# One level of Strassen's scheme for the large products of a streaming encoder layer, in three token groups

## The chip, the cores and the metric

The kernel runs on one core of one Trainium2 chip. The metric is the device time of one execution in microseconds. Three timed runs of the kernel before gave 2399.98, 2401.68 and 2405.52 us, median 2401.68.

## What is computed

One mixer layer over 2048 prompt tokens of one stream and 8 x 16 sample tokens, 1024 channels, all in float32. Cut to what matters:

```python
h = rmsnorm(x, norm_w) * (1.0 + scale) + shift            # scale, shift, gate = silu(c) @ w_ada + b_ada
q, k, v, r, a_lr, u, gv, z, g_a, g_b = split(h @ w_in)     # 1024 x 8208
o, S_new = gla_chunked(q, k, v, log_a, S0)                 # linear attention, 4 heads, carried state
y_a = (rmsnorm(o, gla_norm_w) * silu(r)) @ w_proj_a        # 1024 x 1024
s = mix(layernorm(gv))                                     # 128 x 128 matrices over positions
y_b = (u * s * silu(z)) @ w_proj_b                         # 1024 x 1024
x = x + gate * ((sigmoid(g_a) * y_a + sigmoid(g_b) * y_b) @ w_out)   # 1024 x 1024
y = rmsnorm(x, final_norm_w)
```

The large products are those with `w_in` and the three 1024 x 1024 matrices: 2176 tokens (17 tiles of 128) by 1024 by about 11,264 columns, and 16 columns more for `a_lr`.

## The kernel before, in words

**Split operands.** A float32 product is taken as three products in the format `fp32r`: every operand is split into a rounded `hi` and a rest `lo`, and `hi hi + hi lo + lo hi` is summed in PSUM. For a weight block ACT casts (L177) and DVE or POOL subtracts (L178, `wl<-wr,wh`), in quarters of 128x512.

**Loops.** There are five groups of token tiles (4, 4, 3, 3, 3; the sample tile is in the second). A group goes over all weights once, in 44 blocks of 1024 x 256, so that every weight is loaded and split five times. Two forms of product stand in the code: `nat_slot` (L318 to L320: tokens stationary, 256 weight columns moving; for r, v, gv and the output product) and `tr_slots` (L340 to L342: weights stationary, the group's 384 or 512 tokens moving; for the rest). The group's operands (`h`, the attention output, the gated gMLP product, the merged branches) stay in SBUF, already split.

**Order.** The program is written out in its order by Python. `run_block` cuts a weight block's products in slots of 12 (`nat_slot`) or 6 (`tr_slots`), two or four of which fill a bank; before each slot it lets the queue of side work (`Side`) take one step and gives out a quarter of the next block's split. Side work is the linear attention (`gla_gen`), the position mixing (`smix_gen`), the norm and split of the next group's `h` (`stats_gen`, `h_gen`). Every engine runs its own instructions strictly in the order written. The output of a slot lies in one of three PSUM banks (`psg`) until ACT or DVE has taken it out (the `*_evac` functions).

**Fallback.** `body(tc, io, True)` is the path that runs; a flag computed on the chip decides whether the slower `body(tc, io, False)` repeats everything.

## Time and profile before

| | |
|---|---|
| median of three timed runs | 2401.68 us |
| profiled execution, first to last instruction (span) | 2394.5 us |
| what lies around the span, median less span | 7.2 us |
| PE (matmul) busy | 2328.8 us, 97%, 14928 instructions |
| DVE busy | 1004.0 us, 42%, 1935 |
| ACT busy | 920.9 us, 38%, 2015 |
| POOL busy | 965.8 us, 40%, 1085 |
| DMA | 296.91 MB, mean 124 GB/s |
| mean granted TensorE clock | 0.990 of 2.4 GHz |

The page gives no time of the profiled execution beyond its span, so the median stands for it. Matmul times are modelled and overlap: a product of 256 columns is listed with 290 ns although the next one starts 120 ns later. How dense PE works is therefore read from the starts in a timeline, not from the busy share.

### The profile page before, as it was taken

What the parts mean: (1) busy time and instruction counts of PE and PEld (TensorE: products, weight loads), DVE (VectorE), ACT (ScalarE), POOL (GpSimd) and SP (SyncE); (2) the same over time, 40 slices, a digit from 0 to 9 for tenths busy, and PEclk for the clock granted to TensorE, in tenths of its full rate; (3) what the DMA queues carried; (4) which work ended last, traced back from release to release, by engine and by line L of the source; (5) the groups of instructions that cost most, each with busy time, mean ns of one, the idle gap of its engine ahead of it and who ended that gap; (6) DMA issues with size and microseconds to landing.
All of it is one profiled execution on the core that took longest, in us unless ns stands there. A gap on an engine that the chain in (4) does not pass through costs nothing. (4 is left out here: it accounts for less than half of the span.)

```text
span 2394.5 us, 38041 instructions
## 1 busy us (share of the span) xinstructions
PE 2328.8 (97%) x14928; PEld 2183.6 (91%) x14928; DVE 1004.0 (42%) x1935; ACT 920.9 (38%) x2015; POOL 965.8 (40%) x1085
## 2 busy tenths in 40 slices
PE   6999999999999999999999999999999999999998
PEld 4889988889988878888999999999999999999998
DVE  3356522236367432215456322546523264752323
ACT  3344322333434322333455334445433445533342
POOL 3323323344422222435634344563434365433445
PEclk9999999999999999999999999999999999999999
DMA  7643324443444343444444445554445546443543
GB/s 232 177 103 74 91 95 96 98 144 128 127 108 116 95 126 91 97 126 154 134 106 98 123 117 135 189 142 107 98 123 124 168 150 148 94 115 119 125 141 125
DMA packets 286512, 296.91 MB, mean 124 GB/s; under 512 B 10593, under 2 KB 273561, under 8 KB 286322
## 3 DMA queue, kind: packets, MB, share of 16 engines
q1 hardware_dynamic: 282994, 286.74, 44.4%
q10 hardware_dynamic: 2112, 4.19, 0.5%
q0 software_dynamic: 1216, 3.44, 0.4%
q8 instruction: 119, 1.95, 0.3%
q14 instruction: 71, 0.58, 0.1%
HBM read 277.82 MB, written 16.52 MB: 123 GB/s over the span
## 5 line engine op out<-in xcount | busy, mean ns | idle before, releaser
L178 POOL TENSOR_TENSOR wl<-wr,wh 128x512 fp32r<-128x512 f32 (+1 forms) x440 | 579.2, 1318 | 912.4 <-ACT wh L177 864.4
L340 PE MATMUL pg<-u,wh 128*128 128x384 f32 (+1 forms) x2240 | 809.2, 361 | 2.7 <-DVE redo L1028 2.7
L342 PE MATMUL pg<-u,wl 128*128 128x384 f32 (+1 forms) x2240 | 800.0, 357 | 0.0
L341 PE MATMUL pg<-u,wh 128*128 128x384 f32 (+1 forms) x2240 | 799.4, 357 | 0.0
L318 PE MATMUL pg<-wh,u 128*128 128x256 f32 (+1 forms) x2144 | 622.1, 290 | 0.0
L319 PE MATMUL pg<-wl,u 128*128 128x256 f32 (+1 forms) x2144 | 610.1, 285 | 3.4 <-DVE wl L178 2.1
L320 PE MATMUL pg<-wh,u 128*128 128x256 f32 (+1 forms) x2144 | 609.5, 284 | 0.0
L177 ACT CAST wh<-wr 128x512 fp32r<-128x512 f32 (+1 forms) x880 | 512.5, 618 | 209.3 <-issue 89.3
L178 DVE TENSOR_TENSOR wl<-wr,wh 128x512 fp32r<-128x512 f32 (+1 forms) x440 | 337.7, 768 | 516.8 <-ACT wh L177 513.3
L340 PEld LDWEIGHTS pg<-u,wh 128*128 128x128 f32 x2240 | 421.7, 188 | 37.4 <-issue 4.3
L342 PEld LDWEIGHTS pg<-u,wl 128*128 128x128 f32 x2240 | 421.3, 188 | 35.8
L341 PEld LDWEIGHTS pg<-u,wh 128*128 128x128 f32 x2240 | 421.7, 188 | 33.5 <-issue 0.5
L318 PEld LDWEIGHTS pg<-wh,u 128*128 128x128 f32 x2144 | 412.5, 192 | 6.1 <-issue 3.0
L319 PEld LDWEIGHTS pg<-wl,u 128*128 128x128 f32 x2144 | 413.0, 193 | 5.4 <-DVE wl L178 2.3
L320 PEld LDWEIGHTS pg<-wh,u 128*128 128x128 f32 x2144 | 412.7, 193 | 0.0
L1105 POOL TENSOR_TENSOR s<-s,u 128x128 f32<-128x128 f32 x136 | 76.3, 592 | 67.6 <-ACT s L1102 67.6
L353 POOL TENSOR_SCALAR st<-st 128x1 f32<-128x1 f32 x119 | 29.9, 252 | 150.3 <-ACT s L818 93.3
L1079 ACT ACTIVATE u<-pg,ptf 128x384 f32<-128x384 f32 (+1 forms) x40 | 25.0, 625 | 165.5 <-PE pg L342 165.5
L650 POOL TENSOR_TENSOR u<-u,gnwf 128x256 f32<-128x256 f32 x68 | 56.4, 833 | 72.2 <-ACT u L647 69.8
L1084 DVE TENSOR_TENSOR u<-pg,u 128x384 f32<-128x384 f32 (+1 forms) x40 | 24.4, 611 | 134.7 <-PE pg L342 134.7
L1196 POOL TENSOR_TENSOR u<-u,yt 128x256 f32<-128x256 f32 x67 | 55.0, 824 | 56.7 <-DVE yt L1195 56.6
L177 ACT CAST u<-s 128x384 fp32r<-128x384 f32 (+1 forms) x40 | 22.2, 556 | 138.0 <-DVE s L1112 138.0
(202 smaller groups left out, 1964.7 us busy)
## 6 DMA issues: line engine op xcount, KB each, us to landing
wr<-w_in SPq DMA_DIRECT2D x270, 512.0 KB, 5.2
wr<-w_in SPq DMA_DIRECT2D x80, 256.0 KB, 6.0
wr<-w_proj_a SPq DMA_DIRECT2D x40, 512.0 KB, 3.4
wr<-w_proj_b SPq DMA_DIRECT2D x40, 512.0 KB, 3.4
wr<-w_out SPq DMA_DIRECT2D x40, 512.0 KB, 3.4
u<-x_prompt SPq DMA_DIRECT2D x32, 512.0 KB, 6.2
u<-w_ada SPq DMA_DIRECT2D x16, 512.0 KB, 9.0
o_yp<-u SPq DMA_DIRECT2D x15, 512.0 KB, 3.5
```

What stands on the lines that cost most here:

```text
L177: act.copy(hi, src)
L178: eng.tensor_tensor(lo, src, hi.bitcast(F32), ALU.subtract)
L318: pe.matmul(o, ahi(k)[:, t], hi[:, k, 0:w], start=k == 0, stop=False)
L319: pe.matmul(o, ahi(k)[:, t], lo[:, k, 0:w], start=False, stop=False)
L320: pe.matmul(o, alo(k)[:, t], hi[:, k, 0:w], start=False, stop=k == 7)
L340: pe.matmul(o, hi[:, k, cs], bhi(k), start=k == 0, stop=False)
L341: pe.matmul(o, hi[:, k, cs], blo(k), start=False, stop=False)
L342: pe.matmul(o, lo[:, k, cs], bhi(k), start=False, stop=k == 7)
L353: pool.tensor_scalar(dst, src, scale, EPS, ALU.mult, ALU.add)
L650: pool.tensor_tensor(d, d, gnw, ALU.mult)
L1105: pool.tensor_tensor(tj, tj, gv(j)[:, c * 128:(c + 1) * 128], ALU.mult)
L1196: (dve if last and n == 3 else pool).tensor_tensor(y(j)[:, cs], y(j)[:, cs], t, ALU.add)
```

## The change

The first path is replaced by `fast_body`; the fallback `body(tc, io, False)` stays.

A weight block of 1024 x 256 and a group's operand are cut into halves both in the contraction (even and odd chunks of 128) and in columns or tokens. Winograd's form of Strassen's scheme then needs seven block products in place of eight, and 15 additions: four sums `T1` to `T4` of weight quarters (POOL, L281 to L287), four sums `S1` to `S4` of operand quarters (`combos`, L220 to L229), and seven sums of the products, taken partly in PSUM (later products are added to a bank that already holds an earlier one) and partly by DVE (`evac`, L335 to L339, and the `*_fin` functions).

There are three groups of tiles: 6, 5 (with the sample tile) and 6. All products have weights stationary; half a group's tokens move: 384, 320, 384 columns. A *place* is one of a block's seven products: 12 matmuls into one of the banks R, X, Q. In the program's list of places the first place of a block comes before the last of the block ahead. While place n is issued, the weights of place n+4 are summed, those of n+3 cast and those of n+2 subtracted.

The split operands of a phase (7 quarters and sums, `hi` and `lo`) fill 14 of 18 large tiles, so there is room for one set only. Every operand is therefore written to DRAM as seven float32 sums (`publish`) and, during the last block of the phase ahead, loaded again and split (`build_plan`: 14 pairs of load and fill, 128x768 or 128x640). The gates and the merged first branch also go by way of DRAM. The first group's `h` is summed and split directly in the prologue (`direct`). Between the last projection b and the last output phase, which needs its result, no other phase is left; its operands are built when projection b has ended (`flush`). `v`, `gv` and the output now come out with channels on partitions, and are transposed on PE.

```diff
+AOPS = ("S1", "A11", "S2", "S4", "A12", "S3", "A22")
+BOPS = ("T1", "B11", "T2", "B22", "B21", "T3", "T4")
+PLACE = "RXQRXQQ"
+P_GN, P_NF = 68, 70
+LEAD = 2
...
+    groups = [prompt[0:6], [("s", 0)] + prompt[6:10], prompt[10:16]]
...
+    upool, spool, cpool = pl("u", 18), pl("s", 5), pl("c", 6)
+    rpool, tpool, wpool = pl("wr", 4), pl("wt", 3), pl("w", 6)
...
+    def combos(even, odd, h, eng=None):
+
+        a11, a21, a12, a22 = even[:, 0:h], even[:, h:2 * h], odd[:, 0:h], odd[:, h:2 * h]
+        e = (lambda: eng) if eng is not None else either
+        yield "A11", a11
+        yield "A12", a12
+        yield "A22", a22
+        x1 = CT(h)
+        e().tensor_tensor(x1, a21, a22, ALU.add)
+        yield "S1", x1
+        x2 = CT(h)
+        e().tensor_tensor(x2, x1, a11, ALU.subtract)
+        yield "S2", x2
+        x4 = CT(h)
+        e().tensor_tensor(x4, a12, x2, ALU.subtract)
+        yield "S4", x4
+        x3 = CT(h)
+        e().tensor_tensor(x3, a11, a21, ALU.subtract)
+        yield "S3", x3
+
+    def publish(st, kp, even, odd, eng=pool):
+        for o, src in combos(even, odd, st.h, eng):
+            sync.dma_start(st.d[o, kp // 2][:, kp % 2, :], src)
+            yield
+
...
+        def add(self, o):
+            q, sub = self.quarter, ALU.subtract
+            if o == "T1":
+                pool.tensor_tensor(self.t4(o), q("B12"), q("B11"), sub)
+            elif o == "T2":
+                pool.tensor_tensor(self.t4(o), q("B22"), self.tmp["T1"], sub)
+            elif o == "T3":
+                pool.tensor_tensor(self.t4(o), q("B22"), q("B12"), sub)
+                self.t4("T4")
+                pool.tensor_tensor(self.tmp["T4"], q("B21"), self.tmp["T2"], sub)
+
+        def src(self, o):
+            return self.tmp[o] if o[0] == "T" else self.quarter(o)
+
+        def hi(self, o):
+            self.w[o] = wpool.tile([128, 2, 4, 128], F32R, tag="w", name=nm("w"))
+            act.copy(self.w[o][:, 0], self.src(o))
+
+        def lo(self, o):
+            w = self.w[o]
+            (pool if o == "T3" else dve).tensor_tensor(w[:, 1], self.src(o), w[:, 0].bitcast(F32), ALU.subtract)
+
...
+    def evac(b, i):
+
+        blk, bk = blocks[b], banks[b]
+        h = blk.ops.h
+        if i == 1:
+            bk["p1"], bk["t"] = CT(h), CT(h)
+            act.copy(bk["p1"], bk["X"])
+            dve.tensor_tensor(bk["t"], bk["R"], bk["p1"], ALU.add)
+        elif i == 2:
+            bk["u2"] = CT(h)
+            dve.tensor_tensor(bk["u2"], bk["Q"], bk["p1"], ALU.add)
+        elif i == 3:
+            blk.fin(1, 0, bk["R"], bk["u2"])
+        elif i == 4:
+            blk.fin(0, 0, bk["X"], None)
+        elif i == 5:
+            blk.fin(1, 1, bk["Q"], bk["t"])
+        elif i == 6:
+            blk.fin(0, 1, bk["Q"], bk["p1"])
+            if blk.after:
+                blk.after()
+            del banks[b]
+
+    last = [None]
+
+    def flush():
+        if last[0] is not None:
...
+    def run(n):
+        b, i = places[n]
...
+        flush()
+        if i == 4 and b + 2 < len(blocks):
+            blocks[b + 2].load()
+        prepare(n + LEAD + 2, "add")
+        prepare(n + LEAD + 1, "hi")
+        prepare(n + LEAD, "lo")
+        bk, ops = banks[b], blk.ops
+        h = ops.h
+        p = PLACE[i]
+        if i < 3:
+            bk[p] = PSG()[:, 0:h]
+        out, w = bk[p], blk.w[BOPS[i]]
+        hi, lo = ops.t[AOPS[i]]
+        for k in range(4):
+            kw = {"skip_group_check": i > 2}
+            pe.matmul(out, w[:, 0, k, :], hi[:, k, :], start=i < 3 and k == 0, stop=False, **kw)
+            pe.matmul(out, w[:, 0, k, :], lo[:, k, :], start=False, stop=False, **kw)
+            pe.matmul(out, w[:, 1, k, :], hi[:, k, :], start=False, stop=k == 3, **kw)
+            if k % 2:
+                step()
+        del blk.w[BOPS[i]]
+        last[0] = (b, i)
+
+
+    class Phase:
+        def __init__(self, g, st, blks, spare, flush=False):
...
+    def build_plan(ph):
+
+        out = []
+        for o in AOPS:
+            for q in range(2):
+                def load(o=o, q=q, box={}):
+                    t = S(2 * ph.ops.h).rearrange("p (k t) -> p k t", k=2)
+                    sync.dma_start(t, ph.set.d[o, q])
+                    ph.box[o, q] = t
+
+                def fill(o=o, q=q):
+                    if q == 0:
+                        ph.ops.alloc(o)
+                    ph.ops.fill(o, slice(2 * q, 2 * q + 2), ph.box.pop((o, q)), pool if q else dve)
+                out.append((load, fill))
+        ph.box = {}
...
+            blk.ops = ph.ops
+            blocks.append(blk)
+    held = {ph.first for ph in phases if ph.flush}
+    for b in range(len(blocks)):
+        if b in held:
+            places.append((b - 1, 6))
+        places.append((b, 0))
+        if b and b not in held:
+            places.append((b - 1, 6))
+        places += [(b, i) for i in range(1, 6)]
+    places.append((len(blocks) - 1, 6))
...
         with tc.manual_schedule():
-            body(tc, io, True)
+            fast_body(tc, io)
```

**On PE**, at a switch from one product chain to the next in a product with weights stationary (first group, `pg` is the PSUM bank; `u` the split operand; `wh`, `wl` or `w` the split weights). Before:

```order
L342 MATMUL pg_3867<-u_374,wl_3755 128x512
L340 MATMUL pg_3867<-u_374,wh_3754 128x512
L341 MATMUL pg_3867<-u_376,wh_3754 128x512
L342 MATMUL pg_3867<-u_374,wl_3755 128x512
L340 MATMUL pg_3906<-u_230,wh_3826 128x512
L341 MATMUL pg_3906<-u_232,wh_3826 128x512
```

With the change, where place 6 of one block (`A22` with `T4`, added into bank Q) ends and place 1 of the next (`A11` with `B11`, bank X) begins:

```order
L381 MATMUL pg_5874<-u_720,w_5912 128x384
L382 MATMUL pg_5874<-u_721,w_5912 128x384
L383 MATMUL pg_5874<-u_720,w_5912 128x384
L381 MATMUL pg_5993<-u_470,w_5932 128x384
L382 MATMUL pg_5993<-u_471,w_5932 128x384
L383 MATMUL pg_5993<-u_470,w_5932 128x384
```

A chain of 24 matmuls of 512 columns has become a place of 12 of 384. The first place adds into a bank that DVE has read twice before, and the bank of the second was last read after place 4 of the block ahead.

**On POOL**, in projection b of the first group (`wl`, `w`: `lo` of weights; `wt`: sums of weights; `u_4299` and `u_7910`: the merged branch; `c`: sums for the operand of the output product). Before:

```order
L178 TENSOR_TENSOR wl_4543<-wr_4464,wh_4542 128x512
L1147 TENSOR_TENSOR u_4299<-u_4299,u_3125 128x512
L178 TENSOR_TENSOR wl_4543<-wr_4485,wh_4542 128x512
L1147 TENSOR_TENSOR u_4299<-u_4299,u_3125 128x512
L178 TENSOR_TENSOR wl_4621<-wr_4540,wh_4620 128x512
L1147 TENSOR_TENSOR u_4299<-u_4299,u_3125 128x512
L178 TENSOR_TENSOR wl_4621<-wr_4561,wh_4620 128x512
L1147 TENSOR_TENSOR u_4299<-u_4299,u_3125 128x512
```

With the change (L1194 and L1195 are the gate and the merge, L220 to L229 the operand sums, the others the weights):

```order
L285 TENSOR_TENSOR wt_8102<-wr_7779,wr_7777 128x512
L287 TENSOR_TENSOR wt_8104<-wr_7779,wt_8042 128x512
L281 TENSOR_TENSOR wt_8128<-wr_8021 128x512
L220 TENSOR_TENSOR c_8147<-u_7910 128x384
L298 TENSOR_TENSOR w_8130<-wt_8102,w_8130 128x512
L223 TENSOR_TENSOR c_8161<-c_8147,u_7910 128x384
L226 TENSOR_TENSOR c_8170<-u_7910,c_8161 128x384
L1194 TENSOR_TENSOR u_8059<-u_8059,c_8173 128x384
L1195 TENSOR_TENSOR u_8060<-u_8060,u_8059 128x384
L229 TENSOR_TENSOR c_8190<-u_7910 128x384
L1195 TENSOR_TENSOR u_8060<-u_8060,u_8059 128x384
L283 TENSOR_TENSOR wt_8201<-wr_8023,wt_8128 128x512
```

Between one block's first weight sum (L281) and the next there stood two subtractions and two merges for each slot; now five instructions on weights, seven of the branch and four of the operand sums stand there.

**On DVE**, one token tile's step of the linear attention (first group; `sstf` the state, `am`, `kl`, `sh`, `v` small split operands, `pg` a product's bank). Before:

```order
L890 TENSOR_TENSOR sstf<-pod_1783,sstf 128x256
L891 TENSOR_SCALAR sstf<-sstf,st_1284 128x256
L837 TENSOR_TENSOR am_1805<-pat_1801,kcf 128x128
L178 TENSOR_TENSOR al_1810<-am_1805,ah_1809 128x128
L847 TENSOR_TENSOR kl_1813<-ptr_1803,kn_1807 128x128
L178 TENSOR_TENSOR sl_1835<-sstf,sh_1834 128x256
L178 TENSOR_TENSOR u_1449<-ptr_1838,u_1448 128x2x128
L952 TENSOR_TENSOR x_1616<-pg_1821,x_1615 128x256
L749 SCALAR_TENSOR_TENSOR oa_1860<-pod_1783,st_1794,u_497 128x256
L178 TENSOR_TENSOR wl_1863<-wr_1617,wh_1862 128x512
```

With the change:

```order
L965 TENSOR_TENSOR sstf<-pod_2296,sstf 128x256
L966 TENSOR_SCALAR sstf<-sstf,st_1614 128x256
L903 TENSOR_TENSOR am_2320<-pat_2314,kcf 128x128
L165 TENSOR_TENSOR kl_2323<-ptr_2316,kn_2322 128x128
L165 TENSOR_TENSOR v_2326<-ptr_2316,v_2326 128x256
L165 TENSOR_TENSOR al_2330<-am_2320,ah_2329 128x128
L165 TENSOR_TENSOR sh_2343<-sstf,sh_2343 128x256
L937 SCALAR_TENSOR_TENSOR u_1680<-ptr_2346,ptf,u_1680 128x128 x2
L833 COPY st_2352<-s_2156 128x6
L839 TENSOR_REDUCE st_2354<-s_2155 128x1
L840 TENSOR_TENSOR flagf<-flagf,st_2354 128x1
L298 TENSOR_TENSOR w_2287<-wt_2143,w_2287 128x512
```

Each step has one subtraction more (`v`), and the sums of products (`pg`) and of weights (`w`) stand between the steps on the same queue.

## Rows read from the trace of the kernel before

**Rows 1.** Windows: engines' busy us (instructions), granted clock, DMA share, GB/s, two stretches.

```profile
0.00:55.00 55.00, 37.45 (x236) 24.69 (x236) 18.12 (x34) 19.73 (x38) 17.26 (x30) 0.97 0.76 249
55.00:2384.30 2329.30, 2291.30 (x14693) 2158.93 (x14692) 982.42 (x1897) 900.64 (x1976) 946.66 (x1052) 0.99 0.45 121
```

**Rows 2.** Groups by shape on PE: count | busy, mean ns | idle before.

```profile
L318 PE MATMUL pg<-wh,u 128*128 128x256 f32 x2040 | 592.1, 290 | 0.0
...
L340 PE MATMUL pg<-u,wh 128*128 128x384 f32 x1344 | 455.3, 339 | 2.7 <-DVE redo L1028 2.7
...
L340 PE MATMUL pg<-u,wh 128*128 128x512 f32 x896 | 353.9, 395 | 0.0
```

**Rows 3.** Timeline of PE in three streams: start us, duration us, instruction.

```profile
500.20 0.39 PE L341 MATMUL pg<-u,wh 128*128 128x512 f32 x1
500.43 0.39 PE L342 MATMUL pg<-u,wl 128*128 128x512 f32 x1
...
2002.07 0.28 PE L318 MATMUL pg<-wh,u 128*128 128x256 f32 x1
2002.19 0.28 PE L319 MATMUL pg<-wl,u 128*128 128x256 f32 x1
...
2200.05 0.33 PE L341 MATMUL pg<-u,wh 128*128 128x384 f32 x1
2200.23 0.33 PE L342 MATMUL pg<-u,wl 128*128 128x384 f32 x1
```

**Rows 4.** Timeline of PE around a burst of transposes among products.

```profile
1553.02 0.49 PE L370 MATMUL ptr<-kcf,u 128*128 128x128 f32 x3
1553.27 0.36 PE L318 MATMUL pg<-wh,u 128*128 128x256 f32 x1
```

**Rows 5.** Timeline of PE: two places of the start, and the last product.

```profile
27.03 0.39 PE L474 MATMUL pg<-wh,u 128*128 128x272 f32 x1
...
55.14 0.36 PE L318 MATMUL pg<-wh,u 128*128 128x256 f32 x1
...
2384.07 0.28 PE L320 MATMUL pg<-wh,u 128*128 128x256 f32 x1
```

**Rows 6.** Groups by shape on POOL: count | busy, mean ns | idle before, releaser.

```profile
L178 POOL TENSOR_TENSOR wl<-wr,wh 128x512 fp32r<-128x512 f32 x430 | 562.9, 1311 | 899.5 <-ACT wh L177 851.6 <-PE pg L320 18.8 <-issue 14.7
...
L1196 POOL TENSOR_TENSOR u<-u,yt 128x256 f32<-128x256 f32 x67 | 55.0, 824 | 56.7 <-DVE yt L1195 56.6
L1147 POOL TENSOR_TENSOR u<-u,u 128x384 f32<-128x384 f32 x24 | 33.8, 1408 | 7.9 <-DVE u L1146 7.9
```

**Rows 7.** Groups by shape on DVE and ACT, from the same view.

```profile
L178 DVE TENSOR_TENSOR wl<-wr,wh 128x512 fp32r<-128x512 f32 x430 | 328.6, 764 | 507.3 <-ACT wh L177 503.8
...
L1084 DVE TENSOR_TENSOR u<-pg,u 128x384 f32<-128x384 f32 x24 | 13.4, 557 | 69.6 <-PE pg L342 69.6
...
L177 ACT CAST wh<-wr 128x512 fp32r<-128x512 f32 x860 | 500.4, 617 | 183.1 <-issue 89.3 <-PE pg L341 55.1 <-DMA wr<-w_in 15.2
```

**Rows 8.** Timeline of DVE and POOL where their instructions overlap, and where not.

```profile
510.31 0.68 DVE L178 TENSOR_TENSOR wl<-wr,wh 128x512 fp32r<-128x512 f32 x1
...
510.47 1.66 POOL L1147 TENSOR_TENSOR u<-u,u 128x512 f32<-128x512 f32 x1 [3.07 <-DVE u L1146]
...
385.72 0.97 DVE L178 TENSOR_TENSOR wl<-wr,wh 128x512 fp32r<-128x512 f32 x1 [4.47 <-ACT wh L177]
...
385.25 2.17 POOL L1105 TENSOR_TENSOR s<-s,u 128x128 f32<-128x128 f32 x4 [2.02 <-ACT s L1102]
```

**Rows 9.** Timeline of ACT and DVE in one token tile's step of the linear attention.

```profile
1700.22 0.38 ACT L818 ACTIVATE s<-pod 128x256 bf16<-128x256 f32 x1 [2.12 <-PE pod L184]
...
1702.31 0.28 DVE L847 TENSOR_TENSOR kl<-ptr,kn 128x128 fp32r<-128x128 f32 x1
```

**Rows 10.** DMA issues: count, KB each, us to landing.

```profile
wr<-w_proj_b SPq DMA_DIRECT2D x40, 512.0 KB, 3.4
...
o_yp<-u SPq DMA_DIRECT2D x15, 512.0 KB, 3.5
```

964 lines of the change are left out of this document (added).

## The prediction

> **What bounds the kernel now.** I read the windows first. From 55 us to the last product the matmul unit is busy 2291 of 2329 us at a granted clock of 0.99, that is at the upper of its two levels, 2.4 GHz, while DVE, ACT and POOL are each busy about 40% [rows 1]. Next come the groups by shape [rows 2] and the starts in the timeline [rows 3], because busy times of matmuls overlap: a product of 512 columns starts 0.23 us after the one ahead (0.227 over longer stretches), one of 384 after 0.17 (0.173), one of 256 after 0.12. From counts and steps follows the dense stream: 4032 products of 384 columns (3 x 1344) make 698 us, 2688 of 512 make 610, 6432 of 256 or 272 make 771, together 2079. The stream runs from 55.14 to 2384.07 us [rows 5], so 250 us of it are something else: small products, transposes, and waits. TensorE sets the time, and nine tenths of it is the large products. The last 10 us of the span have none.
>
> **Large products: minus 269.** The scheme has 132 blocks of 7 places of 12 products. 88 blocks move 384 columns: 7392 x 0.173 = 1279 us. 44 move 320, which no row shows; the three steps of rows 3 are 13 to 14 ns above columns divided by 2.4 GHz, so I take 0.147: 3696 x 0.147 = 543. Together 1822, against 2079 and the 96 products done before 55 us (12 us): 2091. Bounds for 320 columns are the steps of 256 and 384: 444 to 639 us.
>
> The Trainium skill (TensorE: Matmul & The Clock Gate, section Back-to-back issue gap) gives the gap as columns over 2.4 GHz plus 2.5 ns, so 136 ns at 320 columns. By that page the term would be 40 us lower; at 256, 384 and 512 columns the rows lie about 11 ns above it in this kernel, so the sum stays with the rows.
>
> **Small work on PE: plus 56.** `v`, `gv` and the output are now transposed: 3 x 68 x 2 = 408 transposes. Three of them take 0.25 us from start to start [rows 4], 0.083 each, and the change back to products costs some more; I take 0.11: 45 us (34 to 60). The low rank product now stands alone: 64 products of 384 and 32 of 320 make 16 us; 17 transposes and the 16 extra columns of before save 5.
>
> **Start: plus 43.** Before, products start at 27 us, beside the conditioning's weights, and at 55.14 one block of 12 us is done [rows 5]: the stream has lost 43 us. Now no place can start before all of `h` of six tiles is there. 3 MB of tokens, 8 MB of `w_ada` and 2 MB of weights at the 249 GB/s of rows 1 land after 52 us; the last quarter then needs transposes, sums and splits, some 14 DVE instructions of about 0.56 [rows 7] in a chain with ACT and PE: 16 us. Behind them, still ahead of the first `evac` on the same queue, stand the sums and splits of the last three operands, of which DVE has 30: 17 us, nearly all lost to the first block. Together 86, so 43 more (20 if the loads hide the chain, 65 if POOL's third of these is the slower one).
>
> **POOL between two groups: plus 58.** For a weight block POOL now makes five instructions of 128x512 at 1.31 us: 6.6 us against a block's 14.5 us on PE (84 x 0.173). That fits. It does not where a group ends. 128x384 lies between 0.82 and 1.31 [rows 6]; I take 1.07 (the row that shows it directly has 1.41, for additions that start beside a DVE subtraction, as in rows 8). Projection b has seven such and its operand sums four more: 6.6 + 11.8 = 18.4 us a block. Fills are seven a phase, 128x768, by the same slope 1.8 us, and 128x640 1.55. The next group's `h` adds 16 sums of 320 columns (0.95), of which many are issued at once where the side queue is drained before projection b. Over the ten blocks from the last gMLP block to the next group's first: weights 66, projections 12.8 + 30, sums 8.6 + 15 + 17, gMLP products 4, three phases of fills 36, together 189 us, against PE's 145 and some 4 of transposes. Of the 40 in excess the weights summed ahead (four places, 8 us) cover 8. The first boundary costs 32, the second less, since four output blocks with little for POOL lie in it: 26. Bounds 10 (0.82, the time of 256 columns, for every 384) to 110 (1.41 for each).
>
> **The held phase: plus 25.** Before the last output phase the chain is: `evac` on DVE 0.56, gate and merge on POOL 2.1, first sum 1.1, a store 3.5 and a load 3.4 [rows 10], cast and subtraction 1.8: 12.5 us without a product. Then 14 fills run at POOL's pace, 7 x 1.8 and the weight sums, against 2.08 us a place: about 12 more. Nothing covers this. Bounds 12 to 35.
>
> **Side chains on DVE and ACT: plus 45.** Before, a finished bank could wait while two more were filled. Now three of seven `evac`s must be done within one place, 2.08 us. In a tile's step of the linear attention ACT and DVE hand work to and fro for 2.4 us, from 1700.22 to 1702.59 [rows 9]; the split of `v` adds about 0.8, and an `evac` behind it in the queue is late by 1 to 2 us in three places of seven: 68 steps x 0.7 = 45. Below: nothing, if the step's own products on PE (9 of 256 columns) cover it; above: 68 x 2 = 136. Queued behind a late `evac` are the `lo` of weights, two places ahead of need.
>
> **Ends.** The last norm needs all four column blocks, six tiles and their stores: plus 10 against the 10 us of before. Of the 38 us in which PE idles within its stream I count 15 as gone with the first form of product.
>
> **Sum.** 2394.5 - 269 + 56 + 43 + 58 + 25 + 45 + 10 - 15 = 2347.5 us of span. The median of the timed runs lies 7.2 above the profiled span; with that 2355 us.
>
> **Rivals.** *B, DVE and POOL block each other.* A DVE subtraction that runs alone beside POOL's later start takes 0.68 us, and POOL's sum that starts 0.16 us into it takes 1.66 in place of 1.31; one that meets two POOL instructions takes 0.97 [rows 8, 6]. So whoever comes second pays about 0.3 to 0.35. With the change both engines are busy about 70% (my sums of instructions by rows 6 and 7: DVE 1600, POOL 1540 us), and nearly all of the 792 `lo` subtractions can meet a POOL instruction. In the linear attention the blocks for `v` and `r` of a head hold 12 of them and some 15 others with two inputs in SBUF: 27 x 0.28 (0.97 less 0.69) is 7.6 us on top of DVE's 38, against PE's 29 and 13 of attention, so 3.6 too much, of which a head hands on 3: 12 heads, 36 us. In the twenty boundary blocks POOL pays 0.375 for seven DVE instructions each: some 50 us. That gives 2355 + 86 = 2441. At half of these meetings it is 2398, no longer distinct from before; that is the point from which it decides. For it: the rows. Against it: over the whole trace POOL's 128x512 subtractions average 1.311 us [rows 6], so most meetings cost little at today's load.
>
> The Trainium skill (SBUF — State Buffer, section Who interferes with whom) states a lock on a port pair shared by VectorE and GpSimd: a VectorE instruction with two SBUF inputs and a GpSimd one that reads SBUF exclude each other, the second blocks. Rows 8 agree in kind; the amount, 0.35 of 0.52 us of overlap, is less than a whole instruction.
>
> *C, all of it hides.* If the queues smooth POOL's excess and the side chains, these 58 and 45 go: 2252. For it: every engine but PE has idle time on average. Against it: the engines run in program order, and the excess stands together.
>
> That the fallback would run is not likely: it does not in the trace of before, and the data are the same.
>
> **Chances.** Forecast 0.50, B 0.28, C 0.22. A difference of 0.2%, 4.8 us, is about what a measurement of this kernel can tell from none. Of the forecast's 0.50, 0.44 are faster, 0.03 the same and 0.03 slower (its own range 2300 to 2405); C is faster; of B 0.25 are slower and 0.03 the same: 0.66 faster, 0.06 the same, 0.28 slower. The range reaches to C's time and past B's: 2250 to 2460. The bounds of the single terms, added up, would reach further on both sides; they don't all fall together.
>
> **What would show it.** Steps of 0.173 and 0.147 us between products in the changed kernel's timeline, and 1822 us in all, show the first term. Products from about 70 us and a pause of some 18 in the first block show the start. PE waiting for POOL's weight sums (`wt`, `w`) near the ends of groups one and two, with POOL at over 90% there, shows the POOL term; PE waiting for DVE behind `am`, `kl`, `v`, `al` shows the side chains; a gap of 12 us before the last output phase shows the held phase. `lo` subtractions with a mean over 0.9 us and POOL sums over 1.5 would mean B. If PE idles under 100 us after its start, C holds. A granted clock much below 0.99 would add time that I counted nowhere.

## The result, and the profile after

The changed kernel takes 2973.03 us in the median of four runs (2969.98 to 2973.75), the kernel before 2400.83 beside it (2399.65 to 2405.52): a ratio of 1.238 with a 95% interval of 1.236 to 1.240. I had forecast 2355 (2250 to 2460). The profiled execution has a span of 2967.8 us, 573 more than before.

From the page of the kernel after, the engines' busy time, and the granted clock in 40 slices of the span (9 is 90% or more of 2.4 GHz):

```profile
PE 2349.5 (79%) x13267; PEld 2204.3 (74%) x13267; DVE 1736.3 (59%) x3026; ACT 1174.6 (40%) x2493; POOL 1711.2 (58%) x1424
...
PEclk7799999999878777878999987879999999988878
```

PE idles for 618 us of the span, and the granted clock, 0.99 before [rows 1], is between 0.7 and 0.9 in many slices. The windows of the kernel after show where (us, busy us and instructions of PE, weight load, DVE, ACT, POOL, clock, DMA share, GB/s). They are the whole stream, which answers to rows 1, the four `gv` blocks of group 0, the linear attention of group 1 with the sample tile, and projection a of group 1:

```profile
55.00:2941.80 2886.80, 2320.16 (x13138) 2189.92 (x13138) 1702.93 (x2940) 1147.75 (x2414) 1698.00 (x1400) 0.89 0.49 122
473.00:535.70 62.70, 62.70 (x375) 62.05 (x374) 35.89 (x62) 27.00 (x58) 28.57 (x22) 1.00 0.56 91
967.50:1314.00 346.50, 255.97 (x1389) 223.35 (x1388) 192.66 (x396) 126.20 (x269) 154.35 (x145) 0.78 0.38 79
1729.70:1870.20 140.50, 76.16 (x398) 70.08 (x397) 80.63 (x131) 50.00 (x121) 70.20 (x56) 0.75 0.60 189
```

In the `gv` blocks PE is never idle and the clock is full; in the other two stretches the clock is 0.78 and 0.75 and PE idles for 91 and 64 us. As a share of the stretch DVE is busy alike in all three, 57, 56 and 57%. Against PE's own busy time it is 57, 75 and 106%. So the scheme runs as forecast where the work beside the products is light for them, and not where it is heavy.

The steps of products, from the timeline of PE in two dense stretches (start, duration, instruction):

```profile
2090.18 0.33 PE L381 MATMUL pg<-u,w 128*128 128x384 f32 x1
2090.35 0.33 PE L382 MATMUL pg<-u,w 128*128 128x384 f32 x1
```

```profile
1200.00 0.31 PE L381 MATMUL pg<-u,w 128*128 128x320 f32 x1
1200.15 0.31 PE L382 MATMUL pg<-u,w 128*128 128x320 f32 x1
```

A product of 384 columns starts 0.173 after the one ahead, as in rows 3, and one of 320 after 0.147: what I had taken from the rows on either side.

**Where the 573 us come from.** I went through all starts on PE. A step counts as work up to the usual step of its line and width at 2.4 GHz (its 30th percentile); what is above it in stretches granted 1.2 GHz, up to 0.85 of the step, is put down to the lower clock, and the rest is waiting. "Ends" is what the span has besides.

| us | before | after | difference | forecast |
|---|---|---|---|---|
| large products | 2089 | 1818 | -271 | -269 |
| other work on PE | 160 | 218 | +58 | +56 |
| lower clock | 12 | 146 | +134 | 0 |
| waits | 118 | 757 | +639 | +156 (43 + 58 + 25 + 45 - 15) |
| ends | 16 | 29 | +13 | +10 |

The work on PE and the ends came out as forecast, to 2 or 3 us each. The waits did not, and beside them stands the lower clock. Of the 757 us, 84 lie before the second block, 232 in the rest of the linear attention, 154 in projections a, 95 in projections b, 49 in the output phases, and 144 in the other blocks of `w_in`.

What PE waited for, in the kernel after (us in total, times, longest):

```profile
PE pg L381 <- DVE c L336: 83.1, 33, 12.2
PE pg L383 <- POOL w L298: 63.0, 31, 5.6
PE pod L986 <- DMA s<-state_gla: 54.5, 13, 10.1
PE pg L381 <- DVE c L1193: 44.9, 5, 12.9
PE ptr L668 <- POOL s L663: 38.6, 1, 38.6
PE pg L381 <- DVE c L1173: 34.9, 9, 10.3
...
PE pg L383 <- DVE w L298: 16.0, 14, 11.7
```

No single cause leads. An `evac` or a `*_fin` on DVE stands behind three of these rows, the subtraction of a weight on POOL and on DVE behind two, the loads of the sample tile's states behind one, and the start's 38.6 us are one wait for a POOL memset. What stands behind a wait for DVE shows in the timelines of DVE and SP at the end of group 0 (start, duration, instruction, idle before it and what ended that):

```profile
948.59 0.83 DVE L165 TENSOR_TENSOR u<-s,u 128x640 fp32r<-128x640 f32 x1 [15.39 <-ACT u L164]
949.34 0.68 DVE L298 TENSOR_TENSOR w<-wt,w 128x512 fp32r<-128x512 f32 x1
949.94 0.55 DVE L1193 TENSOR_TENSOR c<-pg,c 128x384 f32<-128x384 f32 x1
```

```profile
930.26 0.99 SPq L266 DMA_DIRECT2D wr<-w_in  x2
...
934.78 0.44 SPq L1182 DMA_DIRECT2D u<-gb03f  x1
935.27 0.58 SPq L1183 DMA_DIRECT2D u<-m103f  x1
935.91 0.81 SPq L404 DMA_DIRECT2D s<-h1S10f  x1
```

The first operand of the next phase (`h1S1`) is asked for at 935.91, behind a weight block and 1.5 MB of gates, and its fill is the next thing in DVE's program. DVE stands still for 15.39 us until ACT has cast what arrived, and the `evac` (L1193) that the next place needs starts at 949.94, 12.9 us too late for PE. ACT's queue is held in the same way, and with it the `evac` for which PE waits longest in total (L336), since DVE adds there to what ACT has copied (L335). ACT's and DVE's timelines in projection a of group 1:

```profile
1777.30 0.42 ACT L480 ACTIVATE sq<-u 128x256 bf16<-128x256 f32 x1 [20.28 <-DMA u<-x_prompt]
...
1780.85 0.49 DVE L336 TENSOR_TENSOR c<-pg,c 128x320 f32<-128x320 f32 x1 [9.94 <-ACT c L335]
```

The first square of the next group's tokens waits 20.28 us for their load, and the copy behind the squares comes late. Of the 83 us at L336 five waits make 50: two behind such squares, three behind ACT's casts for the fills of projection b. A queue can also be late by its own work. In the wait of PE that is shown next, from 1755.6 to 1765.9, DVE is busy for 8.3 us, most of it with rows of the last norm:

```profile
1762.86 2.46 DVE L1265 SCALAR_TENSOR_TENSOR u<-u,yrs,c 128x256 f32<-128x256 f32 x6 [1.90 <-DMA c<-final_norm_w]
```

What a wait does besides shows on PE:

```profile
1755.25 0.31 PE L383 MATMUL pg<-u,w 128*128 128x320 f32 x1
1765.87 0.61 PE L381 MATMUL pg<-u,w 128*128 128x320 f32 x1 [10.31 <-DVE c L1173]
1766.28 0.47 PE L382 MATMUL pg<-u,w 128*128 128x320 f32 x1
1766.54 0.47 PE L383 MATMUL pg<-u,w 128*128 128x320 f32 x1
...
1768.68 0.41 PE L382 MATMUL pg<-u,w 128*128 128x320 f32 x1
1768.92 0.31 PE L383 MATMUL pg<-u,w 128*128 128x320 f32 x1
```

After 10.3 us without a product the next ones start 0.267 apart, at the lower level of the granted clock, 1.2 GHz; the step is 0.147 again from 1768.92 on.

DVE's `lo` and POOL's sums, by shape (count, busy, mean ns, idle before), answer to rows 6 and 7:

```profile
L298 DVE TENSOR_TENSOR w<-wt,w 128x512 fp32r<-128x512 f32 x396 | 388.1, 984 | 92.2 <-ACT w L294 89.8
L298 DVE TENSOR_TENSOR w<-wr,w 128x512 fp32r<-128x512 f32 x396 | 368.4, 930 | 10.2 <-ACT w L294 10.2
...
L298 POOL TENSOR_TENSOR w<-wt,w 128x512 fp32r<-128x512 f32 x132 | 199.7, 1513 | 172.6 <-ACT w L294 172.6
L285 POOL TENSOR_TENSOR wt<-wr,wr 128x512 f32<-128x512 f32 x132 | 193.4, 1465 | 71.2 <-DVE w L298 70.8
...
L281 POOL TENSOR_TENSOR wt<-wr 128x512 f32<-128x512 f32 x132 | 178.3, 1351 | 83.0 <-issue 27.6 <-PE pg L383 22.9 <-DVE w L298 18.7
```

The mean of `lo` is 0.96 us for 0.76 before [rows 7], that of POOL's four sums 1.42.

### The profile page after: what moved, and what is told of

Read it like the earlier page. It is cut to its first block, busy times and chain, and to the rows that moved or that the text cites. A ratio compares the mean times of both kernels' runs of the same rounds, so it can differ in the third digit from the quotient of the medians.

```text
span 2967.8 us, 38482 instructions
## 1 busy us (share of the span) xinstructions
PE 2349.5 (79%) x13267; PEld 2204.3 (74%) x13267; DVE 1736.3 (59%) x3026; ACT 1174.6 (40%) x2493; POOL 1711.2 (58%) x1424
## 5 line engine op out<-in xcount | busy, mean ns | idle before, releaser
L381 PE MATMUL pg<-u,w 128*128 128x384 f32 (+1 forms) x3696 | 1297.8, 351 | 269.3 <-DVE c L336 83.1
L383 PE MATMUL pg<-u,w 128*128 128x384 f32 (+1 forms) x3696 | 1256.8, 340 | 79.1 <-POOL w L298 63.0
L382 PE MATMUL pg<-u,w 128*128 128x384 f32 (+1 forms) x3696 | 1251.5, 339 | 0.8 <-DVE u L165 0.8
L381 PEld LDWEIGHTS pg<-u,w 128*128 128x128 f32 x3696 | 734.2, 199 | 307.6 <-DVE c L336 94.0
L383 PEld LDWEIGHTS pg<-u,w 128*128 128x128 f32 x3696 | 731.6, 198 | 95.1 <-POOL w L298 74.3
L382 PEld LDWEIGHTS pg<-u,w 128*128 128x128 f32 x3696 | 734.3, 199 | 2.4 <-DVE u L165 1.5
L294 ACT CAST w<-wt 128x512 fp32r<-128x512 f32 x528 | 318.6, 617 | 436.1 <-POOL wt L283 213.6
L298 DVE TENSOR_TENSOR w<-wt,w 128x512 fp32r<-128x512 f32 x396 | 388.1, 984 | 92.2 <-ACT w L294 89.8
L298 DVE TENSOR_TENSOR w<-wr,w 128x512 fp32r<-128x512 f32 x396 | 368.4, 930 | 10.2 <-ACT w L294 10.2
L298 POOL TENSOR_TENSOR w<-wt,w 128x512 fp32r<-128x512 f32 x132 | 199.7, 1513 | 172.6 <-ACT w L294 172.6
L294 ACT CAST w<-wr 128x512 fp32r<-128x512 f32 x396 | 239.1, 614 | 5.7 <-PE pg L383 5.0
L285 POOL TENSOR_TENSOR wt<-wr,wr 128x512 f32<-128x512 f32 x132 | 193.4, 1465 | 71.2 <-DVE w L298 70.8
L281 POOL TENSOR_TENSOR wt<-wr 128x512 f32<-128x512 f32 x132 | 178.3, 1351 | 83.0 <-issue 27.6
L287 POOL TENSOR_TENSOR wt<-wr,wt 128x512 f32<-128x512 f32 x132 | 192.5, 1459 | 16.7 <-DVE w L298 15.3
L164 ACT CAST u<-s 128x768 fp32r<-128x768 f32 (+1 forms) x154 | 118.9, 792 | 200.4 <-DMA s<-mg2S10f 11.7
L283 POOL TENSOR_TENSOR wt<-wr,wt 128x512 f32<-128x512 f32 x132 | 183.8, 1392 | 3.2
L336 DVE TENSOR_TENSOR c<-pg,c 128x384 f32<-128x384 f32 (+1 forms) x132 | 70.2, 532 | 139.0 <-ACT c L335 118.7
L335 ACT COPY c<-pg 128x384 f32<-128x384 f32 (+1 forms) x132 | 60.5, 458 | 115.5 <-PE pg L383 106.3
```

The lines of the kernel that those rows point to most:

```text
L164: act.copy(hi, src)
L281: pool.tensor_tensor(self.t4(o), q("B12"), q("B11"), sub)
L283: pool.tensor_tensor(self.t4(o), q("B22"), self.tmp["T1"], sub)
L285: pool.tensor_tensor(self.t4(o), q("B22"), q("B12"), sub)
L287: pool.tensor_tensor(self.tmp["T4"], q("B21"), self.tmp["T2"], sub)
L294: act.copy(self.w[o][:, 0], self.src(o))
```

## The experiments

A span is that of the run's profile, and the columns are those of the table above. Line numbers in rows of these runs are those of their own programs, a few lines off. Large products (1817 to 1819), other work (208 to 220) and ends (28 to 30) hardly differ, so the two columns that do stand here.

| run | span | waits | lower clock |
|---|---|---|---|
| changed kernel | 2968 | 757 | 146 |
| e1 operands from a resident tile | 2890 | 685 | 145 |
| e2 loads in place and early | 2890 | 692 | 137 |
| e3 weight sums on DVE | 2875 | 680 | 134 |
| e4 four changes of order | 2764 | 596 | 111 |
| e5 longer time for an `evac`, alone | 2945 | 718 | 161 |
| e6 e4 + e3 + e5 | 2621 | 488 | 72 |
| e7 e6, next group's `h` spread out | 2632 | 495 | 78 |
| e8 only T3's subtraction on DVE | 2916 | 711 | 141 |
| e9 e4 + e3 | 2661 | 514 | 82 |
| e10 e6, weights a place earlier | 2615 | 484 | 76 |
| e11 e10, two sums back on POOL | 2649 | 511 | 83 |
| e12 changed kernel without weight work | 2623 | 474 | 89 |
| e13 e10 without weight work | 2385 | 281 | 43 |

**e1 and e2: do the loads at a change of phase hold the queues?**

```diff
 # e1
-    sync.dma_start(t, ph.set.d[o, q]); ph.box[o, q] = t
+    ph.box[o, q] = kc[:, 0:ph.ops.h].unsqueeze(1).broadcast_to([128, 2, ph.ops.h])
 # e2: load into the lo tile; the fill comes three places later
+    sync.dma_start(ph.ops.t[o][1][:, 2 * q:2 * q + 2, :].bitcast(F32), ph.set.d[o, q])
+    ph.ops.fill(o, ks, ph.ops.t[o][1][:, ks, :].bitcast(F32), pool if q else dve)
```

> Left out: the loads of the operands at the changes of phase. Each fill reads a tile that is in SBUF from the start (the values are other ones); the fills' own instructions on ACT, DVE and POOL, the sums and the stores stay. Theory A (fills that wait for their loads hold the queues of ACT, DVE and POOL, the evac behind them comes late, PE idles and the granted clock falls): the blocks on both sides of the eleven changes of phase lose about 355 us above the pace of the products, of which 150 to 250 are loads, so 2720 to 2820 us for the profiled span of 2968, clock about 0.91. Rival B (DVE and POOL block each other): both keep their instructions, so the time falls by less than 60 us, over 2910.

> Same computation. An operand is loaded straight into its lo tile and split there, the load is issued as soon as the old operand's tiles are free and the fill three places later, so no fill is queued right behind its own load. Theory A: most of what the run without loads gains, 2740 to 2860 us, and no wait of DVE or POOL over 5 us at the changes of phase but the last one. Rival B: within 40 us of the changed kernel, over 2930.

Both took 2889.5 us of span, 78 less. The mechanism is there, and placing the loads better wins as much as leaving them out. But it is worth half of the least that I expected of e1. In the 22 blocks on either side of the eleven changes of phase PE's waits fall from 266 us to 193 in e1 and 182 in e2, so most of the waiting there is for other things. My sign for e2, no wait of DVE over 5 us there except at the last change, did not come: its waits for a cast reach 8.8. ACT's wait for the next group's tokens, 20.3 us above, stays in both, at 21.

**e3 and e8: the weight sums on POOL.**

```diff
 # e3: all five; e8: the last line alone
-                pool.tensor_tensor(self.t4(o), q("B12"), q("B11"), sub)
+                dve.tensor_tensor(self.t4(o), q("B12"), q("B11"), sub)
...
-            (pool if o == "T3" else dve).tensor_tensor(w[:, 1], self.src(o), w[:, 0].bitcast(F32), ALU.subtract)
+            dve.tensor_tensor(w[:, 1], self.src(o), w[:, 0].bitcast(F32), ALU.subtract)
```

> Same computation. The four sums of a weight block and the subtraction of T3 move from POOL to DVE. Rival B: POOL's load halves, the lo subtractions go back from 0.96 us to about 0.70 and the 86 us that I priced for B go: under 2890. Theory A: DVE gets 528 sums of 0.7 us and 132 subtractions more, 74% busy for 59%, the waits for POOL's w (63 us) go and those for evac grow: 2930 to 3010.

> Same computation as the changed kernel; of the five instructions that POOL does for a weight block only the last, the subtraction of T3, moves to DVE (132 of 1.51 us become 132 of about 0.96). It tells apart why the run with all five on DVE won 96 us. Queue: a place waits for the subtraction that stands last in POOL's queue (63 us of waits), so without it most of the 96 us come here too: 2880 to 2920 us. Rival B (the lock of DVE and POOL): the sums stay on POOL and DVE gets more to do beside them, so nothing: 2950 to 2990.

e3 took 2874.8, 93 less, so my theory A missed and rival B's number came true. e8 took 2915.9: 52 of the 93 come with the one subtraction that stands last in POOL's queue. Groups by shape of e3, then of e8:

```profile
L298 DVE TENSOR_TENSOR w<-wt,w 128x512 fp32r<-128x512 f32 x528 | 440.9, 835 | 15.8 <-ACT w L294 15.6
...
L298 DVE TENSOR_TENSOR w<-wr,w 128x512 fp32r<-128x512 f32 x396 | 342.5, 865 | 6.6 <-ACT w L294 6.6
```

```profile
L298 DVE TENSOR_TENSOR w<-wt,w 128x512 fp32r<-128x512 f32 x528 | 502.5, 955 | 108.7 <-ACT w L294 108.4
...
L298 DVE TENSOR_TENSOR w<-wr,w 128x512 fp32r<-128x512 f32 x396 | 366.8, 926 | 11.2 <-ACT w L294 11.2
```

In e8 `lo` is as slow as in the changed kernel, 0.94 on average, and still 52 us went. So they are hardly a matter of blocking, but of where the subtraction stands and of the 1.51 us that it takes there, as the queue theory had it. With the sums away from POOL `lo` falls to 0.85, not to the 0.68 of a subtraction alone [rows 8]. The other 41 us are what the blocking of DVE and POOL and POOL's slower additions cost together, less what DVE's added work costs. The runs do not split them, so the 41 are no upper bound for B, to which I gave 86.

**e4: the order of the side work.** e2, and three changes beside it:

```diff
 # states of the sample tile: two loads at a head's start, not eight into two buffers
+                    sync.dma_start(s8, io["state_gla"][0, 4 * half:4 * half + 4, hh].rearrange("b k v -> k b v"))
 # start: an operand's own sum alone
-            for kp in range(3):
-                direct(kp, (o,))
+                    either().tensor_tensor(src, ev[:, 0:hh], ev[:, hh:2 * hh], ALU.subtract)
 # scans, squares, scales, row norms: a step of the side queue for every two or three;
 # the next group's squares and the position matrices' memset come some steps later
+                if j % 2:
+                    yield
```

> Same computation, four changes of order alone: operands loaded in place and early (as above), the states of the sample tile loaded in two pieces at a head's start, sums at the start not computed again for each operand, and the side work (squares, row norms, scans) given out two or three instructions at a time in place of six. Theory A: of the 757 us that PE waits and the 146 us lost at the lower clock the changes of phase give back 180, the sample tile 100, the start 35, the side work 80: 2570 us (2480 to 2680). Rival B: none of this lowers the load of DVE or POOL, over 2850.

A time of 2767.47 us (ratio to the kernel before 1.152, 1.149 to 1.156), 206 less than the changed kernel, where 400 were expected. The blocks tell the parts: group 1's attention, with the sample tile, fell from 345 to 281 us, the first block from 67 to 44. These are 64 and 23 us where I had 100 and 35. The loads alone brought 78 (e2) for 180, which leaves some 40 of the 204 in span for the rest of the side work, for 80. The parts are not runs of their own, and may overlap. ACT's wait for the next group's tokens falls from 20.3 us to 2.8, and PE's waits for the `evac` behind it (L336) from 83 to 43.

**e5: is one place too little for an `evac`?**

```diff
-AOPS = ("S1", "A11", "S2", "S4", "A12", "S3", "A22")
-PLACE = "RXQRXQQ"
+AOPS = ("S1", "A11", "S2", "A12", "S4", "S3", "A22")
+PLACE = "RXQXRQQ"
-    psg = pl("psg", 3, bass.MemoryType.PSUM)
+    psg = pl("psg", 4, bass.MemoryType.PSUM)
-        places.append((b, 0))
+        places += [(b, 0), (b, 1)]
```

> Same computation as the changed kernel, with more time for an evac: the products on X come before those on R, a fourth bank for products (the attention's small scores share the transposes' banks), and the last place of a block moves behind the second place of the next, so each evac that DVE takes part in has two places and not one. Theory C (the waits are short ones, an evac late by 1 to 2 us within one place of 2.08 us, as my term for the side chains had it): the 330 us that PE waits for evac and copies nearly go, and half of the lower clock's 146: 2600 to 2720 us. Theory A (the evacs stand behind instructions that themselves wait 3 to 12 us): 2 us more at some 80 such waits, so 100 us with the clock: 2830 to 2910.

A span of 2945.2: 23 us, less than either theory. What PE waited for in e5:

```profile
PE pg L382 <- DVE w L297: 113.9, 64, 10.8
PE pg L382 <- POOL w L297: 70.6, 29, 6.1
PE pod L985 <- DMA s<-state_gla: 47.9, 14, 7.1
PE ptr L934 <- DVE am L902: 46.0, 36, 3.2
```

The waits for `evac` on DVE left the head of the list, and the waits for `lo` on DVE, 16 us before, are 114: the same late queue is waited for at another instruction. But the edit brings a wait of its own. It lets the attention's small scores share the transposes' banks, and the 46 us for `am` in the last row do not stand among the changed kernel's waits. So 23 us is what the longer time wins less what the shared banks cost, and the run does not show that the time of a place is worth no more.

**e6, e7, e9: together.**

> Same computation: the four changes of order of the run that reached 2767 us, the weight sums on DVE and the longer time for an evac, together. If the gains add (about 95 for the sums, 100 for the evacs): 2570 us (2500 to 2640). If they are one and the same waits, won once: over 2680.

> As the run before, and the next group's tokens are normed and summed over the whole of projections a and b in place of being finished at once where projection b begins. In the run with four changes of order the blocks of projections a and b of groups 0 and 1 still waited 148 us; theory A says that the burst there is about a third of it: 2510 us (2440 to 2590). If the burst is nothing, the same as the run before.

> Same computation: the four changes of order and the weight sums on DVE, without the longer time for an evac. If the longer time is worth 26 us here as it was alone: 2650 us. If it matters only once the queues hold few long waits, this run stays over 2690 and so over half of the 144 us between the two runs is the evac's.

e9 2660.7, e6 2621.4: with e4's order the sums on DVE win 103 us, and the longer time for an `evac` 39 on top, for 23 alone. The gains add and a little more. The shared banks cost in e6 too: its waits for `am` are 24 us. Spreading the next group's `h` (e7: 2631.27 us, ratio 1.096, 1.094 to 1.098) won nothing; my theory of a burst there fell.

**e10 and e11: what is left.**

```diff
-LEAD = 2
+LEAD = 3
 # e10 also gives the side queue a step for every square of a token tile
 # e11: T1 and T3 on POOL, T2 and T4 and all lo on DVE
```

> Same computation: the run of 2623 us, with a weight block prepared one place earlier (three places ahead of its use) and one square of a token tile at a time given to ACT. Of that run's waits 131 us are for DVE's w and 12.8 us once for the tokens of the next group. If the waits for w are those of a queue that is busy in bursts, one more place takes half or more of them, with the clock: 2540 us (2480 to 2590). If DVE is short of time on average (78% busy), they only move: over 2600.

> As the run before, but T1 and T3, the two sums that need no other sum, stay on POOL and T2, T4 go to DVE. If DVE's time is short: 30 to 60 us less than the run before. If the lock of DVE and POOL takes what DVE is spared, or T2 and T4 now wait for POOL in DVE's queue: equal to it or more.

From the page and the waits of e10:

```profile
PE 2263.7 (87%) x13267; PEld 2147.6 (82%) x13267; DVE 2042.5 (78%) x3664; ACT 1173.4 (45%) x2493; POOL 814.4 (31%) x754
```

```profile
PE pg L382 <- DVE w L297: 41.6, 25, 7.2
PE ptr L487 <- issue: 24.4, 7, 15.1
PE ptr L939 <- DVE am L907: 24.0, 25, 1.7
PE pg L380 <- DVE c L1198: 20.7, 10, 5.3
```

The waits for `w` fell from 131 to 42 us, and the time did not: 2619.98 us (ratio 1.093, 1.091 to 1.095) for the 2623 of one run of e6. Of the 89 us that left, 53 came back as waits for other instructions of DVE, which is 78% busy, 15 for ACT and 17 for POOL. Giving POOL two of the sums back cost 34 us.

**e12 and e13: the load itself.** The first block's seven prepared weight tiles are kept and used by all others (here and in e1 the flag that could start the fallback is held at zero):

```diff
-        if 0 <= n < len(places):
+        if 0 <= n < len(places) and places[n][0] == 0:
...
-        out, w = bk[p], blk.w[BOPS[i]]
+        out, w = bk[p], blocks[0].w[BOPS[i]]
-        dve.tensor_scalar(io["redo"], low[0:1, :], 1.0, None, ALU.add)
+        dve.tensor_scalar(io["redo"], low[0:1, :], 0.0, None, ALU.mult)
```

> Left out: loading and preparing the weights of all blocks but the first; every block multiplies with the first block's seven weight tiles. Products, evacs, fills, sums of operands and side work are those of the changed kernel. Theory F (DVE, ACT and POOL have more in their queues, in stretches, than PE's time lets them do, and what stands in front of an evac there is weight work): DVE loses 757 of its 1736 busy us, POOL 948 of 1711, ACT 558 of 1175, and the 757 us of waits fall to about 350 with the clock's 146 to 70: 2480 us (2400 to 2560). Theory G (the waits are chains of single hand-overs, each as long whatever the load): over 2700.

> Left out: the same weight work, here in the run of 2617 us (order of side work, loads and fills changed, longer time for an evac). Theory F: of its 484 us of waits and 76 of lower clock 250 stay: 2310 us (2250 to 2400), under the kernel before, so the scheme's own products, evacs and operands would have fitted. Theory G: over 2500.

From e12 the page and PE's first wait, then e13's page and a window of e13, most of the `z` and `u` blocks of group 0:

```profile
PE 2247.8 (86%) x13267; PEld 2150.0 (82%) x13267; DVE 984.4 (38%) x2240; ACT 690.4 (26%) x1576; POOL 701.0 (27%) x769
```

```profile
PE pg L379 <- DVE c L336: 75.0, 35, 11.8
```

```profile
PE 2192.6 (92%) x13267; PEld 2107.5 (88%) x13267; DVE 1000.7 (42%) x2223; ACT 691.5 (29%) x1576; POOL 700.0 (29%) x754
```

```profile
600.00:716.00 116.00, 116.00 (x669) 115.73 (x669) 37.28 (x55) 31.92 (x73) 57.62 (x48) 1.00 0.48 162
```

Spans of 2622.8 and 2384.8. Order, loads, time for an `evac` and place of the sums (e10) take 353 us off the changed kernel; no weight work (e12) takes 345; both (e13) take 583. The two overlap by 115, and neither is the cause alone. In the window of e13 PE is never idle, as in the `gv` blocks above. Theory F holds for e13 and forecast too much for e12, where 474 us of waits stay with DVE at 38% and POOL at 27%: a queue that is mostly empty still keeps PE waiting for an `evac`, up to 11.8 us in the row above. Both runs leave out the loads of the weights as well (231.0 MB moved for 368.7), so they do not tell the weights' work on DVE, ACT and POOL from their traffic, behind which other loads stand. And e13 has all of the scheme's products, evacs and operands and no weight to prepare, and is only 8 us below the kernel before, in one run each (2386.68 and 2395.09). So in this order of the side work even no weight work at all wins no more than that, and no run of the full computation beats the kernel before; the best takes 2620.

## Why the prediction was wrong, step by step

- **Large products, -269: right.** 1822 us forecast, 1818 measured, at steps of 0.173 and 0.147. The Trainium skill (TensorE: Matmul & The Clock Gate, Back-to-back issue gap) gives columns over 2.4 GHz plus 2.5 ns for an isolated product, 136 ns at 320 columns; the rows of this stream show 147.
- **Small work on PE, +56: right**; it measured 58.
- **Ends, +10, and the held phase, +25: right.** Before the last output phase PE waits 14.8 us for the first cast and 11.7 in the first place, 26.5 in all. The 11.7 are one wait for a weight's `lo`, which stands on DVE behind its seven fills. The waits of PE from 2841 to 2942 us:

```profile
PE pg L381 <- ACT u L164: 14.8, 1, 14.8
PE pg L383 <- DVE w L298: 11.7, 1, 11.7
```

- **Start, +43: the place right, the size not.** The first product came at 71.7 us (70 forecast). The waits in the first block are 44 us for the 18 that I counted. My count of DVE's instructions for the last operands, 30, is right, but they take it 29 us, from 79.2 to 108.1, and not 17: it waits for POOL's sums between them, and many take longer than 0.56. (In e4, which does not compute the sums again for each operand, the block is 23 us shorter.) Not in my count is that the transposes of the position matrices stand in PE's queue inside that block, behind a memset that waits for their load. SP's timeline shows it asked for at 113.28, behind the store of the small low rank weights; PE goes on at 117.85. DVE's last subtraction of a weight ahead of the first `evac` starts at 114.34 and takes 0.69, so by an estimate from these rows the transposes add some 3 to 5 us:

```profile
112.41 0.34 SPq L645 DMA_DIRECT2D waldf<-u  x1
...
113.28 0.90 SPq L656 DMA_DIRECT2D s<-w_s  x1
```

- **POOL between two groups, +58: there, but smaller, and not what PE mostly waits for.** In the ten blocks of the first boundary (720.6 to 1004.3 us) PE's waits for POOL's `w` are 19.6 us for 32 forecast, from the last gMLP block of group 1 to the first block of group 2 they are 20.7 for 26. In projection b of group 0, from 873.6 to 967.5, POOL is busy 78 of 94 us, 83% and not over 90. But all of PE's waits in these two stretches are 105 and 145 us. The longest are for DVE, behind fills whose loads had just been asked for. I had priced POOL's instructions at a change of phase and taken the 14 loads for done. A load is asked for at most three fills ahead, one and a half places or 3 us, and the first right before its fill; `h1S1` took some 11 us, from 935.91 to the cast ahead of 948.59.
- **Side chains on DVE and ACT, +45: this is the step that failed.** I had 68 steps of the attention by 0.7 us (48, not the 45 that I wrote), an `evac` late by 1 to 2 us in three places of seven, and wrote "Queued behind a late `evac` are the `lo` of weights, two places ahead of need", as if that were harmless. For a late `evac` in the attention the size is not far off: in gaps over 0.3 us PE waits there 60 us for DVE at L336 and L742. The error is that the term ended there. The attention has 232 us of waits beyond its first block, 44 of them for the loads of the sample tile's states, which I put at nothing. The 144 us in the other blocks of `w_in` I put at nothing too, and the 249 in the projections I priced with POOL's 58. (The kernel before has 118 us of waits in all.) An engine's queue is late by what stands first in it and waits, 3 to 20 us (e1, e2, the timelines of DVE and ACT), and by what it carries (the last norm's rows; e12, together with the weights' loads), and everything behind it is late by as much: `evac` or, given time for that, `lo` (e5, e10). The slack of a place, on which I spent the term, won 23 to 39 us in these runs, after what the shared banks cost.
- **The granted clock: left out.** The prediction said that a clock below 0.99 would add time counted nowhere; it added 134 us. It falls with the waits from 146 beside 757 over 111 beside 596 and 76 beside 484 to 43 beside 281, though not in step with them: e5 has 161 beside 718. No run had one without the other.
- **Rival B** had its first sign (`lo` over 0.9) and not its second (sums over 1.5; they are at 1.42). What can be told of its price is the 41 us between e8 and e3, which hold other things both ways; how much of the 639 it is stays open. The rule of the Trainium skill that I cited for it (SBUF — State Buffer, Who interferes with whom) agrees in kind: `lo` is 0.96 beside POOL's sums and 0.85 without them. **Rival C** fell: after 55 us PE idles for 567 us, not under 100.

What is not settled: how the remaining 484 us of e10 divide. 140 lie in the attention, 178 in the projections, 44 at the start; e13 says that about 203 of them need the weight work and the weights' loads to be there, and no run separates DVE's part from ACT's, POOL's and the loads'.

## What to carry to other kernels

A scheme that saves TensorE an eighth of its products and gives the engines beside it more to do must be costed on their queues, not on their busy shares. At about 40% busy DVE, ACT and POOL hid their work behind the products [rows 1]; at 59, 40 and 58%, with loads awaited inside the queues, they kept PE waiting for 757 us. Look in each engine's program for the instruction that waits longest (a fill behind its own load, a cast behind another engine's sum), charge its wait to everything queued behind it, and add what the clock loses after such gaps.

## What the runs showed that I had not expected

A wait on PE costs more than itself: 146 us at 1.2 GHz beside 757 of waits in the changed kernel, a fifth on top. Giving an `evac` twice the time won 23 us of 757 (e5): waits for `lo` in the same queue rose by 98, and those for `am`, new with the shared banks, are 46. And moving four sums and a subtraction from POOL, 58% busy, to DVE, 59% busy, made the kernel faster by 93 to 103 us (e3, e9): POOL's subtraction of 128x512 takes 1.51 us and DVE's 0.85 in e3.
